# The mixers' output product: sixteen column products replaced by four column pairs in the seven-product scheme

## The chip, the cores and the metric

One core of one Trainium2 chip runs the kernel. The metric is the device time of one execution in microseconds (us); less is better. A core has five engines that run side by side, each through its own list of instructions in order: PE (TensorE, matrix products), DVE (VectorE), ACT (ScalarE), POOL (GpSimd) and SP (SyncE, which here only issues transfers). They wait for each other by semaphores.

## What is computed

One layer of a diffusion backbone over 1024 latent tokens and 256 context tokens, width 1024: a SwiGLU feed-forward half-step, then two mixers in parallel (a gated short convolution and grouped-query attention), merged by gates and sent through one output product, then a second feed-forward half-step. Cut to what matters here:

```python
x = x + 0.5 * ml[2] * swiglu(modulate(rms_norm(x, norm1_g), ml[0], ml[1]), ffn1_w_in, ffn1_w_out)
# mixers
merged = g_conv * (y_conv @ w_branch_conv) + g_attn * (o_attn @ w_branch_attn)     # 1024 x 1024
x = x + ml[5] * (merged @ w_out)                                                   # w_out 1024 x 1024
x = x + 0.5 * ml[8] * swiglu(modulate(rms_norm(x, norm3_g), ml[6], ml[7]), ffn2_w_in, ffn2_w_out)
return rms_norm(x, final_g)
```

The change concerns `merged @ w_out` and what stands just before and behind it.

## The kernel before

**Precision.** A float32 operand is split into two parts of a shorter format: the high part is a cast on ACT, the low part (the operand minus its high part) a subtraction on DVE. The function `split` issues both. A product of two operands is three matmuls: high by high, high by low, low by high (`mm3`, `terms`). Every matmul named below takes a 128x128 stationary operand and a 128x512 moving one.

**Layout.** Activations lie with their 1024 features in eight blocks of 128 partitions (index d, j or k) and their tokens in two halves of 512 columns, C0 and C1.

**The seven-product scheme.** The class `Winograd` multiplies a pair of 128-wide output columns of a weight (`pairs`) with both feature halves and both token halves in seven products instead of eight. Each product is 4 blocks x 3 matmuls = 12. The left operands (weights) are made in the generator `lefts`: it loads a raw tile of 512 KB per column (tag `raw`, three buffers), forms sums s1, s2, s3 and a second s2 on POOL, and splits each operand into a tile with the tag `wl` (four buffers). `prefetch` and `left` take from it. The right operands are eight lists `r[i]` of four tiles. Products 1 and 2 need only C0 (`norm0` makes `r[1]`, `r[2]` from the normalised C0: multiply by the broadcast of the norm on DVE into `h`, shift and scale on ACT, split). Products 6, 7, 4, 5, 3 need C1 too (`norm1`). `start` runs products 1 and 2 of the first nine pairs ahead (`AH3`), while `norm1` is made. The feed-forward inputs and the mixers' input use this class; the second feed-forward's instance is named `fast`.

**The stage in question**, after the attention heads, in the program's order:

1. `merge(j, ch)` for j = 0..7 and both halves: 24 matmuls of `w_ba` (the attention branch's weight) with the attention output (`o_parts`, tiles `oh` and `ol`), then on DVE `ga = ga * ps`, `ga = ga + z`, and a split into `m_hi`, `m_lo` (tiles `mh`, `ml`). The weight of one j is loaded and split once and kept for both halves. Two merges of C0 run between the last attention steps.
2. The output product: for C0 then C1, for each d, the weight column `w_out[:, d]` is loaded and split (`load_cols`: one 512 KB load, one ACT cast and one DVE subtraction of 128x1024), 8 x 3 = 24 matmuls follow, and one DVE operation adds the gated result to the residual `x` (tile `x2`, loaded from `xd`). So it has 2 x 8 x 24 = 384 matmuls.
3. `first = fast.norm0()` is stepped after the outputs d = 0, 1 and 2 of C1, so the norm of C0 and the right operands `r[1]`, `r[2]` of the second feed-forward are made while PE still has the outputs of C1 to do. `fast.square(d)` collects the squares of C1.

**Order.** A scheduler with its own model of times sets each engine's order when the program is built; the orders shown below are what it made. Buffers (38 tiles of 4 KB per partition in `apool`, 11 small ones in `tpool`) are handed on when their last reader is done.

Of the kernel before, what the change touches and what calls it, by code (L numbers as in the profile page):

```python
# [9 lines left out]
F32 = mybir.dt.float32  # L10
F32R = mybir.dt.float32r
# [38 lines left out]
def tile_dit_layer(  # L50
# [415 lines left out]
    class Winograd:  # L466
# [103 lines left out]

        def lefts(self, pairs, side_from):

            def cols(src):
                t = wpool.tile([P, SLOT], F32, tag="raw", name=uniq("raw"), bufs=3)
                load(t[:].rearrange("p (k n) -> p k n", n=P), src.rearrange("(k p) n -> p k n", p=P))
                return t[:, :512], t[:, 512:]
# [9 lines left out]
            def parts(src):  # L586
                tag = "wh" if self.side_from and self.n_left in WH else "wl"
                self.n_left += 1
                t = wpool.tile([P, 2, 512], F32R, tag=tag, name=uniq(tag), bufs=W_BUFS)
                split(src, t[:, 0], t[:, 1], self.lo_eng)  # L590
                return t
# [159 lines left out]
        def third(self, u, v):  # L751
# [5 lines left out]
            return u, v  # L757

# [727 lines left out]
    o_parts = [None] * NQ  # L1486

    def split_output(hd, *chunks):
        if o_parts[hd] is None:
            o_parts[hd] = atile("oh", dt=F32R), atile("ol", dt=F32R)  # L1490
        a, b = chunks[0][1], chunks[-1][1] + 512
        split(q_f[hd][:, a:b], *(t[:, a:b] for t in o_parts[hd]))
# [88 lines left out]
    m_hi, m_lo = {}, {}  # L1581
    wa = {}

    def merge(j, ch):

        if j not in m_hi:
            m_hi[j], m_lo[j] = atile("mh", dt=F32R), atile("ml", dt=F32R)
        if j not in wa:
            wa[j] = load_cols(w_ba[0], j * P)
        w, o = wa[j], ch[1]  # L1590
# [5 lines left out]
            (w[0][:, k], w[1][:, k], *(t[:, o : o + 512] for t in o_parts[k])) for k in range(KD)  # L1596
# [6 lines left out]
        dve.tensor_add(out=ga, in0=ga, in1=z)  # L1603
        split(ga, m_hi[j][:, o : o + 512], m_lo[j][:, o : o + 512])
# [265 lines left out]
```

## Time and profile before

| | |
|---|---|
| median of 3 runs | 2720.67 us (2720.63 to 2721.49) |
| the profiled execution | 2717.89 us, its span 2716.1 us |
| mean granted PE clock | 0.991 of full |
| PE busy | 2647.6 us (97%) |
| DVE / ACT / POOL busy | 2006.6 / 1167.2 / 532.1 us |

The profile is one execution. Its span runs from the first to the last instruction; the execution lasts 1.8 us longer than that, and the median run 2.8 us longer than the execution. Matmuls overlap each other, so a matmul's own duration is longer than the step from one start to the next; the step is what counts.

### The profile page before, as it was taken

Reading aid. Unit: us, or ns where it says so; the run is one execution under the profiler, and the core shown is the slowest. Engines: PE = TensorE matmul, PEld = TensorE weight load, DVE = VectorE, ACT = ScalarE, POOL = GpSimd, SP = SyncE. Lnnn points to the kernel's source line nnn. Section 1 sums busy time; section 2 is a strip of 40 time slices with the busy share of each in tenths; the row PEclk is TensorE's granted clock in tenths of the full one; section 3 lists DMA queues with packets and bytes.
Section 4 is the critical chain, followed back from the end, with each engine's and each line's share of the span. In section 5 each row is a group of like instructions: output and inputs, shape, how many; then the busy total and the mean of one; then the engine's idle time right before and its main releaser. Section 6 shows DMA issues by size and latency. Waiting matters only on the chain.

```text
span 2716.1 us, 37388 instructions
## 1 busy us (share of the span) xinstructions
PE 2647.6 (97%) x13593; PEld 2236.8 (82%) x13593; DVE 2006.6 (74%) x3356; ACT 1167.2 (43%) x2317; POOL 532.1 (20%) x409
## 2 busy tenths in 40 slices
PE   7999899999999999999999999999999999999998
PEld 4788798888778877888999888877888888888888
DVE  5889666988787899888478576685548876667885
ACT  5633443333443542333245665674226333334443
POOL 1244001221010043333033111100000442330100
PEclk9999999999999999999999999999999999999998
DMA  7665553445984345433312321001533552227831
GB/s 264 212 195 170 166 168 100 147 129 179 324 206 105 113 151 186 135 118 120 109 32 87 97 82 43 28 32 47 175 105 124 179 163 93 86 89 283 183 86 63
DMA packets 369922, 364.85 MB, mean 134 GB/s; under 512 B 27831, under 2 KB 261449, under 8 KB 369737
## 3 DMA queue, kind: packets, MB, share of 16 engines
q1 hardware_dynamic: 360712, 345.17, 38.5%
q0 software_dynamic: 9024, 17.30, 4.0%
q8 instruction: 106, 1.74, 0.3%
q14 instruction: 80, 0.65, 0.1%
HBM read 296.30 MB, written 66.06 MB: 133 GB/s over the span
## 4 chain that ended last, share of the span: by engine, by line
PE 55%; DVE 3%; ACT 1%; issue 0%; DMA 0%; DVEq 0%; ACTq 0%
PE ps L88 45%; PE pt L88 5%; PE po L88 4%; DVE xb L88 0%; DVE ol L88 0%; ACT pts L88 0%; DVE pts L88 0%; DVE wl L88 0%; DVE x L88 0%; DVE r L88 0%; ACT pl L88 0%; DMA y<-yd 0%; ACT q L88 0%; ACT oh L88 0%; DVE t L88 0%
## 5 line engine op out<-in xcount | busy, mean ns | idle before, releaser
L88 PE MATMUL ps<-r,wl 128*128 128x512 f32 x5232 | 1208.9, 391 | 14.9 <-ACT wl L88 7.9
L88 PEld LDWEIGHTS ps<-r,wl 128*128 128x128 f32 x5232 | 979.8, 188 | 223.1 <-ACT wl L88 10.0
L88 ACT CAST wl<-raw 128x512 fp32r<-128x512 f32 x286 | 176.9, 620 | 291.2 <-PE ps L88 191.6
L88 POOL TENSOR_TENSOR s<-raw 128x512 f32<-128x512 f32 x64 | 95.5, 1492 | 1011.0 <-DMA raw<-in_ffn_w_in_dram 641.7
L88 ACT CAST wl<-s 128x512 fp32r<-128x512 f32 x256 | 158.0, 620 | 315.1 <-PE ps L88 233.4
L88 DVE TENSOR_TENSOR wl<-raw,wl 128x512 fp32r<-128x512 f32 x284 | 198.6, 700 | 80.8 <-ACT wl L88 77.0
L88 DVE TENSOR_TENSOR wl<-s,wl 128x512 fp32r<-128x512 f32 x256 | 230.3, 900 | 12.6 <-ACT wl L88 11.6
L88 POOL TENSOR_TENSOR s<-raw,s 128x512 f32<-128x512 f32 x64 | 107.3, 1677 | 355.2 <-DVE wl L88 347.3
L88 DVE SCALAR_TENSOR_TENSOR macc<-rawm,silu_c,macc 128x512 f32<-128x512 f32 x168 | 141.0, 855 | 8.5 <-DMA rawm<-in_w_mod_dram 7.4
L88 PE MATMUL ps<-wh,r 128*128 128x256 f32 x768 | 141.6, 285 | 0.0
L88 DVE TENSOR_TENSOR pts<-pt,pts 128x512 fp32r<-128x512 f32 x160 | 108.8, 687 | 39.3 <-ACT pts L88 38.3
L88 DVE TENSOR_REDUCE m<-ps 128x1 f32<-128x512 f32 (+1 forms) x192 | 110.9, 596 | 31.1 <-PE ps L88 30.3
L88 DVE TENSOR_TENSOR u<-u,ps 128x512 f32<-128x512 f32 x168 | 114.1, 679 | 23.2 <-PE ps L88 22.9
L88 ACT CAST pts<-pt 128x512 fp32r<-128x512 f32 x160 | 93.2, 593 | 88.6 <-PE pt L88 86.7
L88 PE MATMUL ps<-rh,wl 128*128 128x512 f32 x360 | 123.7, 395 | 3.9 <-ACT rh L88 3.9
L88 ACT CAST rh<-hid 128x512 fp32r<-128x512 f32 x132 | 81.0, 620 | 103.4 <-PE ps L88 86.3
L88 PEld LDWEIGHTS ps<-wh,r 128*128 128x128 f32 x768 | 120.6, 192 | 0.0
L88 ACT CAST wh<-raw 128x512 fp32r<-128x512 f32 (+1 forms) x88 | 69.4, 796 | 100.5 <-PE ps L88 73.0
L88 PE MATMUL po<-pts,vh 128*128 128x512 f32 x256 | 110.6, 438 | 1.5 <-ACT pts L88 1.5
L88 PE MATMUL ps<-wl,r 128*128 128x256 f32 x384 | 108.8, 283 | 0.0
L88 DVE TENSOR_TENSOR rl<-hid,rh 128x512 fp32r<-128x512 f32 x132 | 89.9, 686 | 23.8 <-ACT rh L88 11.4
L88 PE MATMUL ps<-kl,qs 128*128 128x512 f32 x384 | 105.3, 397 | 0.0
(295 smaller groups left out, 5082.0 us busy)
## 6 DMA issues: line engine op xcount, KB each, us to landing
raw<-in_ffn_w_in_dram SPq DMA_DIRECT2D x125, 512.0 KB
raw<-in_ffn_w_out_dram SPq DMA_DIRECT2D x72, 512.0 KB
rawm<-in_w_mod_dram SPq DMA_DIRECT2D x128, 256.0 KB
raw<-in_w_in_dram SPq DMA_DIRECT2D x61, 512.0 KB
hid<-hd SPq DMA_DIRECT2D x40, 512.0 KB
ws<-in_ffn_w_out_dram POOLq DMA_DIRECT2D x30, 512.0 KB, 6.6
ucd<-uc SPq DMA_DIRECT2D x22, 512.0 KB
hd<-c SPq DMA_DIRECT2D x38, 256.0 KB
```

What stands on the lines that cost most here:

```text
L88: inst = getattr(self.engine, name)(*args, **kw)
```

## The change

- A class `OutColumns(Winograd)` computes `merged @ w_out` as four pairs of output columns in the seven-product scheme: 4 x 7 x 12 = 336 matmuls.
- The right operands are made inside `merge`. A merge of C0 writes a tile `h0` and splits it into `r[1]` or `r[2]`. Merges run all of C0 first, then C1 in the order 0, 4, 1, 5, 2, 6, 3, 7. After each second one of C1 DVE forms four differences (t1 to t4) and five splits follow (`r[6]`, `r[7]`, `r[4]`, `r[5]`, `r[3]`). Each merge loads and splits its own `w_ba` column, so 16 loads instead of 8.
- The left operands come from a `lefts` of its own: the four `wa` columns first (products 1 and 2 of all pairs), then per pair `wa` and `wb` again with four POOL sums. s1 and the second s2 of the pairs 1 and 2 go to the tag `wh`, to be used later.
- The products stand in the order: 1 and 2 of pairs 0 to 3 (`firsts`), then 6, 7, 4, 5, 3 of pair 0 (`seconds`, `thirds`), 6, 7, 4 of pairs 1, 2 and 3, then 5 and 3 of pairs 1, 2 and 3. Numbered in that order they are called p0 to p27 below.
- The results are added to `x2` per d and half as they come (`add2`), each with its square. The last result of C0 (d = 7) comes from p21. `fast.norm0()` is stepped behind `thirds(1)`, `thirds(2)` and `thirds(3)`.
- Attention outputs are split per half (`o_parts[hd, ch]`) instead of both halves at once for heads 0 to 6.

```diff
+        def part(self, src, tag="wl"):
+            t = wpool.tile([P, 2, 512], F32R, tag=tag, name=uniq(tag), bufs=W_BUFS)
+            split(src, t[:, 0], t[:, 1], self.lo_eng)
+            return t
...
+    class OutColumns(Winograd):
...
+        def lefts(self, pairs, side_from):
+
+            part, late = self.part, []
+            for wa, _ in pairs:
+                yield from map(part, self.cols(wa))
+            for j, (wa, wb) in enumerate(pairs):
+                a, b = self.cols(wa), self.cols(wb)
+                s1, s2, s3 = ttile("s1"), ttile("s2"), ttile("s3")
+                pool.tensor_add(out=s1, in0=b[0], in1=b[1])
+                pool.tensor_sub(out=s2, in0=s1, in1=a[0])
+                pool.tensor_sub(out=s3, in0=a[0], in1=b[0])
+                yield part(s2)
+                yield part(s3)
+                yield part(b[1])
+                pool.tensor_sub(out=s2, in0=a[1], in1=s2)
+                if 0 < j < len(pairs) - 1:
+                    late += part(s1, "wh"), part(s2, "wh")
+                else:
+                    yield from late if j else ()
+                    yield part(s1)
+                    yield part(s2)
...
+        def given(self, k, i, ch):
+
+            if ch == C0:
+                self.keep(1 + i, k, self.h0[k][:, i])
+            elif i:
+                f, h, t34, t1, t2 = self.h0[k], self.h1[k], atile("t34", (P, 2, 512)), ttile("nt"), ttile("nt")
+                b12, b22, t3, t4 = h[:, 0], h[:, 1], t34[:, 0], t34[:, 1]
+                dve.tensor_sub(out=t1, in0=b12, in1=f[:, 0])
+                dve.tensor_sub(out=t2, in0=b22, in1=t1)
+                self.keep(6, k, t2)
+                dve.tensor_sub(out=t3, in0=b22, in1=b12)
+                dve.tensor_sub(out=t4, in0=t2, in1=f[:, 1])
+                for r, t in ((7, t3), (4, t4), (5, t1), (3, b22)):
+                    self.keep(r, k, t)
...
     def merge(j, ch):
...
-        if j not in wa:
-            wa[j] = load_cols(w_ba[0], j * P)
-        w, o = wa[j], ch[1]
+        w, o = load_cols(w_ba[0], j * P), ch[1]
...
-        dve.tensor_add(out=ga, in0=ga, in1=z)
-        split(ga, m_hi[j][:, o : o + 512], m_lo[j][:, o : o + 512])
+        dve.tensor_add(out=merged.place(j % 4, j // 4, ch), in0=ga, in1=z)
+        merged.given(j % 4, j // 4, ch)
...
-    for j in range(KD):
-        for ch in (C0, C1):
-            if (j, ch) not in ((0, C0), (1, C0)):
-                run(merge(j, ch))
...
+    for j in range(2, KD):
+        run(merge(j, C0))
+    for j in (0, 4, 1, 5, 2, 6, 3):
+        run(merge(j, C1))
+    merged.prefetch(2)
+    run(merge(7, C1))
...
-    for ch in (C0, C1):
-        o = ch[1]
-        for d in range(KD):
-            w = load_cols(w_out[0], d * P)
-            load(xs(d, ch), xd[d, :, o : o + 512])
-            ps = ps_s()
-            mm3(ps, [
-                (w[0][:, k], w[1][:, k], m_hi[k][:, o : o + 512], m_lo[k][:, o : o + 512]) for k in range(KD)
-            ])
-            dve.scalar_tensor_tensor(
-                out=xs(d, ch), in0=ps, scalar=modl[:, 40 + d : 41 + d], in1=xs(d, ch), op0=ALU.mult, op1=ALU.add
-            )
-            if ch == C1:
-                fast.square(d)
-                if d in (0, 1):
-                    run(first, 1)
-                if d == 2:
-                    run(first)
+    def add2(d, ch, t):
+        load(xs(d, ch), xd[d, :, ch[1] : ch[1] + 512])
+        dve.scalar_tensor_tensor(
+            out=xs(d, ch), in0=t, scalar=modl[:, 40 + d : 41 + d], in1=xs(d, ch), op0=ALU.mult, op1=ALU.add
+        )
+        fast.square(d, ch)
...
+    run(merged.firsts())
+    for j in range(4):
+        add2(2 * j, C0, merged.uc[j][1])
+        add2(2 * j + 1, C0, merged.seconds(j))
+        if j == 0:
+            thirds(0)
+    thirds(1)
+    run(first, 1)
+    thirds(2)
+    run(first, 1)
+    thirds(3)
+    run(first)
```

**How the order moves, PE at the end of the stage.** Names: `ps` is a product's bank, `r` a right operand, `wl` a left one, `pt<-ident,rs_y` the broadcast of the norm of C0, on which `norm0`'s block waits. Before, the broadcast and, behind a row of output products, the last matmuls of the output product with the first ones of the second feed-forward:

```order
L88 MATMUL pt_19113<-ident,rs_y_19064 128x128 x4
...
L88 MATMUL ps_19314<-mh_18616,wh_19308 128x512
L88 MATMUL ps_19314<-ml_18617,wh_19308 128x512
L88 MATMUL ps_19314<-mh_18616,wl_19309 128x512
L88 MATMUL ps_19361<-r_3425_19124,wl_19347 128x512 x3
L88 MATMUL ps_19361<-r_3426_19129,wl_19347 128x512 x3
L88 MATMUL ps_19361<-r_3427_19134,wl_19347 128x512 x3
```

Now (p27 is `ps_19480`):

```order
L88 MATMUL ps_19480<-r_3388_18727,wl_19394 128x512 x3
L88 MATMUL ps_19480<-r_3412_18832,wl_19394 128x512 x3
L88 MATMUL pt_19436<-ident,rs_y_19382 128x128 x4
L88 MATMUL ps_19542<-r_3527_19447,wl_19528 128x512 x3
L88 MATMUL ps_19542<-r_3528_19452,wl_19528 128x512 x3
L88 MATMUL ps_19542<-r_3529_19457,wl_19528 128x512 x3
L88 MATMUL ps_19542<-r_3530_19462,wl_19528 128x512
L88 MATMUL ps_19584<-r_3535_19505,wl_19531 128x512
L88 MATMUL ps_19602<-r_3527_19447,wl_19536 128x512 x3
```

The broadcast stood 75 matmuls ahead of the second feed-forward's first; now it stands directly ahead of it.

**DVE at the same place.** `h<-x,pt` is the norm's multiplication, `r<-h,r` the low part of a right operand, `wl<-raw,wl` that of a left one. Before:

```order
L88 TENSOR_TENSOR h_3421_19118<-x_3357_18699,pt_19113 128x512
L88 SCALAR_TENSOR_TENSOR x_3393_18967<-ps_19206,modl,x_3393_18967 128x512
L88 TENSOR_TENSOR wl_19347<-raw_19345,wl_19347 128x512
L88 TENSOR_TENSOR h_3422_19119<-x_3362_18733,pt_19113 128x512
L88 TENSOR_TENSOR r_3425_19124<-h_3421_19118,r_3425_19124 128x512
L88 TENSOR_TENSOR h_3423_19120<-x_3367_18767,pt_19113 128x512
L88 TENSOR_TENSOR r_3426_19129<-h_3422_19119,r_3426_19129 128x512
L88 TENSOR_TENSOR h_3424_19121<-x_3372_18801,pt_19113 128x512
...
L88 TENSOR_TENSOR r_3427_19134<-h_3423_19120,r_3427_19134 128x512
```

Now:

```order
L88 TENSOR_TENSOR uc_18959<-uc_18959,ps_19480 128x512
L88 TENSOR_TENSOR h_3523_19441<-x_3442_18994,pt_19436 128x512
L88 TENSOR_TENSOR wl_19539<-raw_19534,wl_19539 128x512
L88 SCALAR_TENSOR_TENSOR x_3509_19359<-uc_18959,modl,x_3509_19359 128x512
L88 TENSOR_TENSOR h_3524_19442<-x_3456_19062,pt_19436 128x512
L88 TENSOR_TENSOR r_3527_19447<-h_3523_19441,r_3527_19447 128x512
L88 TENSOR_TENSOR sq_acc_19106<-sq_acc_19106,sq_19496 128x512
L88 TENSOR_TENSOR h_3525_19443<-x_3466_19114,pt_19436 128x512
L88 TENSOR_TENSOR r_3528_19452<-h_3524_19442,r_3528_19452 128x512
L88 TENSOR_TENSOR h_3526_19444<-x_3482_19189,pt_19436 128x512
...
L88 TENSOR_TENSOR r_3529_19457<-h_3525_19443,r_3529_19457 128x512
```

The block has the same shape (from the first `h` to the third low part `r` are 14 instructions in both), but it now stands behind the addition of the last product p27.

**DVE in the middle of the stage**, where left operands are made. Before (`wl<-raw,wh` is the low part of a whole output column's weight, `x<-ps` the addition of a result):

```order
L88 SCALAR_TENSOR_TENSOR x_3357_18699<-ps_18701,modl,x_3357_18699 128x512
L88 TENSOR_TENSOR wl_18831<-raw_18829,wh_18830 128x1024
L88 SCALAR_TENSOR_TENSOR x_3362_18733<-ps_18735,modl,x_3362_18733 128x512
L88 TENSOR_TENSOR wl_18864<-raw_18862,wh_18863 128x1024
L88 SCALAR_TENSOR_TENSOR x_3367_18767<-ps_18769,modl,x_3367_18767 128x512
```

Now, for pairs 2 and 3 (`ps_19158` is p14, `ps_19238` p17, `wl_19138` the left operand of p16, `wl_19218` that of p19; `s` are POOL's sums):

```order
L88 TENSOR_TENSOR wh_19202<-s_3473_19132,wh_19202 128x512
L88 TENSOR_TENSOR uc_18877<-uc_18877,ps_19158 128x512
L88 TENSOR_TENSOR wl_19138<-s_3474_19133,wl_19138 128x512
...
L88 TENSOR_TENSOR uc_18914<-uc_18914,ps_19238 128x512
L88 TENSOR_TENSOR wl_19218<-s_3491_19213,wl_19218 128x512
L88 TENSOR_TENSOR wl_19235<-s_3492_19214,wl_19235 128x512
```

A left operand now stands behind POOL's sums and behind the results of products two before it; SP's list has the loads of `x2` (thirteen, 256 KB each) between the raw columns of pair 1 and the second raw column of pair 2.

More of the change, by code (lines that the diff above doesn't have):

```diff
@@ L1481, in tile_dit_layer @@
     conv_weights(3)
-    o_parts = [None] * NQ
+    o_parts = {}
     def split_output(hd, *chunks):
[L1489 to L1492, printed above, removed]
+        for ch in chunks:
+            t = o_parts[hd, ch] = atile("o", (P, 2, 512), F32R)
+            split(q_f[hd][:, ch[1] : ch[1] + 512], t[:, 0], t[:, 1])
     class Unit:
@@ L1579, in seconds @@
             yield
[L1581 to L1582 removed]
+    merged = OutColumns([tuple(w_out[0][:, d * P : (d + 1) * P] for d in (e, e + 1)) for e in range(0, KD, 2)])
     def merge(j, ch):
[L1586 to L1590 removed]
+        w, o = load_cols(w_ba[0], j * P), ch[1]
         ga, z = ttile("ga"), ttile("z")
@@ L1595, in merge @@
         terms = [
-            (w[0][:, k], w[1][:, k], *(t[:, o : o + 512] for t in o_parts[k])) for k in range(KD)
+            (w[0][:, k], w[1][:, k], o_parts[k, ch][:, 0], o_parts[k, ch][:, 1]) for k in range(KD)
         ]
```

39 lines of the change are left out of this document (32 added, 7 removed).

## The prediction

> **What bounds the kernel now.** I read the page first, then the engines' busy time by stage, then the order of time of PE, DVE and ACT around the output product.
>
> ```profile
> span 2716.1 us, 37388 instructions
> PE 2647.6 (97%) x13593; PEld 2236.8 (82%) x13593; DVE 2006.6 (74%) x3356; ACT 1167.2 (43%) x2317; POOL 532.1 (20%) x409
> PE 55%; DVE 3%; ACT 1%; issue 0%; DMA 0%; DVEq 0%; ACTq 0%
> ```
>
> PE is busy for 97% of the span and carries the chain of work that ended last. Whether that holds in the stage itself is told by a table of three stretches: the merges, the output product, and the products that the second feed-forward runs ahead.
>
> ```profile
> core 0: us, PE busy (x) PEld busy (x) DVE busy (x) ACT busy (x) POOL busy (x), PEclk, DMA share, GB/s
> 1900.00:1964.00 64.00, 64.00 (x284) 53.01 (x283) 33.89 (x46) 15.35 (x20) 0.00 (x0) 1.00 0.49 158
> 1964.00:2052.00 88.00, 88.00 (x395) 73.00 (x394) 47.85 (x70) 32.55 (x45) 0.00 (x0) 1.00 0.36 113
> 2052.00:2102.00 50.00, 50.00 (x232) 41.65 (x231) 41.82 (x72) 29.75 (x51) 4.62 (x3) 1.00 0.42 137
> ```
>
> PE has no gap in any of them, at full clock (1.00), while DVE, ACT and the transfers have room. So a matmul less is time less, as long as PE does not come to wait. What one matmul costs is the step between starts. These rows are PE's in order of time: the last of the merges, the output product's first, one 29 later, the output product's last, and the second feed-forward's first.
>
> ```profile
> 1964.02 0.39 PE L88 MATMUL ps<-oh,wl 128*128 128x512 f32 x1
> 1964.24 0.39 PE L88 MATMUL ps<-mh,wh 128*128 128x512 f32 x1
> 1970.82 0.39 PE L88 MATMUL ps<-mh,wl 128*128 128x512 f32 x1
> 2052.48 0.39 PE L88 MATMUL ps<-mh,wl 128*128 128x512 f32 x1
> 2052.70 1.07 PE L88 MATMUL ps<-r,wl 128*128 128x512 f32 x4
> ```
>
> (1970.82 - 1964.24) / 29 = 0.227 us. A matmul shows 0.39 us of its own because they overlap. And between the output product and the next stage there is no seam: 2052.48 to 2052.70 is one step.
>
> **The change, part by part.**
>
> *Matmuls.* 384 become 336, so 48 steps of 0.227 us go: **-10.9 us**, all of it on PE's path.
>
> *The norm of C0 loses its cover: the first large term.* Before, its block on DVE and ACT ran beside output products. Rows of PE, DVE and ACT in order of time:
>
> ```profile
> 2035.24 0.60 PE L88 MATMUL pt<-ident,rs_y 128*128 128x128 f32 x4
> 2035.87 0.69 DVE L88 TENSOR_TENSOR h<-x,pt 128x512 f32<-128x512 f32 x1 [3.12 <-PE pt L88]
> 2037.10 0.81 ACT L88 ACTIVATE h<-h,modl,gain_l 128x512 f32<-128x512 f32 x1
> 2037.94 0.62 ACT L88 CAST r<-h 128x512 fp32r<-128x512 f32 x1
> 2038.56 0.82 ACT L88 ACTIVATE h<-h,modl,gain_l 128x512 f32<-128x512 f32 x1
> 2038.60 0.69 DVE L88 TENSOR_TENSOR r<-h,r 128x512 fp32r<-128x512 f32 x1
> 2040.67 3.07 DVE L88 TENSOR_TENSOR h<-x,pt 128x512 f32<-128x512 f32 x5
> 2044.32 0.68 DVE L88 TENSOR_TENSOR r<-h,r 128x512 fp32r<-128x512 f32 x1
> 2049.94 0.69 DVE L88 TENSOR_TENSOR r<-h,r 128x512 fp32r<-128x512 f32 x1
> 1964.44 0.69 DVE L88 TENSOR_TENSOR ga<-ga,ps 128x512 f32<-128x512 f32 x1 [2.65 <-PE ps L88]
> ```
>
> The first `h` comes 0.63 us after the broadcast starts; the third low part (2044.32) is done 2045.00 - 2035.87 = 9.13 us after the first `h` starts; the eighth and last (2049.94) 14.76 us after. Between broadcast and the next stage there were 17.5 us, so PE never noticed. Now the order puts the broadcast behind the last output product p27 and directly ahead of the products that need the block. Let 0 be the start of p27's last matmul. DVE adds p27's result first: 0.42 us after that start (1964.02 to 1964.44), for a step of 0.60 (five `h` in 3.07). So the first `h` starts at 1.02 (the broadcast alone would allow 0.23 + 0.63 = 0.86). DVE's list from there to the third low part has 14 instructions in both kernels (a square's sum stands for one addition to `x`), so I take the measured 9.13: third low part at 10.15. PE's list after p27 is: 4 transposes, then 3 matmuls for each of the first two pieces, the third piece's high part, and then its low part. So PE can do 0.23 + 0.36 + 7 x 0.227 = 2.2 us of work and stands for 10.15 - 2.2 = **8.0 us** in pieces. Behind that come 26 matmuls and 8 tiny ones before the eighth low part is wanted, at 10.15 + 26 x 0.227 = 16.0 us at the earliest; it is there at 1.02 + 14.76 = 15.8. So there is one wait, not two. Lower bound: 14 DVE steps of 0.60 without any wait for ACT give the third low part at 9.5, so 7.3 us. Upper bound: a block slower by 1 us, which the spare 0.2 us at its end does not absorb, 9.
>
> *What the wait does to the clock.* The trace has such waits elsewhere; rows of PE in order of time and of the busy time by stretch:
>
> ```profile
> 304.20 2.08 PE L88 MATMUL ps<-hidc,wo 128*128 128x256 f32 x8 [8.98 <-ACT wo L88]
> 308.00:310.00 2.00, 2.00 (x12) 2.00 (x12) 0.43 (x1) 0.62 (x1) 0.00 (x0) 0.61 0.00 0
> 1076.98 15.75 PE L88 MATMUL ps<-r,wl 128*128 128x512 f32 x60 [4.35 <-ACT wl L88]
> 1077.00:1078.00 1.00, 0.97 (x3) 0.52 (x4) 1.00 (x3) 1.00 (x3) 0.22 (x1) 0.79 0.68 262
> 1079.00:1080.00 1.00, 1.00 (x3) 0.77 (x3) 1.00 (x3) 0.01 (x1) 0.07 (x1) 0.50 0.01 2
> 1080.00:1081.00 1.00, 1.00 (x4) 0.75 (x3) 1.00 (x4) 0.00 (x0) 0.00 (x0) 0.51 0.63 182
> 1083.00:1084.00 1.00, 1.00 (x6) 0.79 (x6) 1.00 (x2) 0.00 (x0) 0.00 (x0) 1.00 1.06 323
> 973.00:974.00 1.00, 0.85 (x2) 0.13 (x1) 1.00 (x3) 1.00 (x3) 0.00 (x0) 0.50 0.00 0
> ```
>
> After 4.35 us of idleness the granted clock was 0.79, 0.50, 0.50, 0.51 in the next four microseconds, then 1.00: 0.21 + 0.50 + 0.50 + 0.49 = 1.7 us lost. After 8.98 us it was 0.50 from before the restart at 304.2 until about 309.2: 5.0 us at half speed, 2.5 lost. At 973 two matmuls between two waits ran at 0.50, so single matmuls do not hold the clock up. I take **+1.9 us** (nearest to the 4.35 case, since seven matmuls are spread over the wait; 0 and 2.6 are the ends). [...]
>
> *Left operands and POOL.* Pairs 1 to 3 now want three products (36 steps, 8.2 us) per two raw loads and four POOL sums. The second feed-forward runs the same making of operands at 19 us a pair. Rows of POOL and DVE in order of time, and of the busy time in one stretch:
>
> ```profile
> 2111.97 1.81 POOL L88 TENSOR_TENSOR s<-raw 128x512 f32<-128x512 f32 x1 [4.11 <-DMA raw<-in_ffn_w_in_dram]
> 2123.36 1.70 POOL L88 TENSOR_TENSOR s<-raw 128x512 f32<-128x512 f32 x1 [3.87 <-DMA raw<-in_ffn_w_in_dram]
> 2135.45 1.83 POOL L88 TENSOR_TENSOR s<-raw 128x512 f32<-128x512 f32 x1 [4.79 <-DMA raw<-in_ffn_w_in_dram]
> 2107.23 1.18 DVE L88 TENSOR_TENSOR wl<-raw,wl 128x512 fp32r<-128x512 f32 x1
> 1965.78 1.22 DVE L88 TENSOR_TENSOR wl<-raw,wh 128x1024 fp32r<-128x1024 f32 x1
> 2100.00:2120.00 20.00, 19.77 (x87) 15.73 (x86) 20.00 (x30) 13.13 (x24) 9.08 (x5) 1.00 0.46 156
> ```
>
> The ring of three raw buffers turns in 11.4 to 12.1 us there (2111.97, 2123.36, 2135.45): from the end of the second s2 it takes 3.9 to 4.8 us until the next pair's s1 starts. Working along the lists from p0's start (a product is 2.72 us): pair 0's b column can load when p1's operand buffer is free, at about 7, so s1 at 11.5; its buffer ring gives pair 1's s1 at 22 and s2 at 25 where p13 starts at 35.4: 9 us in hand. Pair 2's b column waits for pair 1's second s2 (30.5), so s2 is done at 38 to 39.6; its low part stands on DVE behind p14's result (41.0) and is ready at 42.3; p16 starts at 43.5. The second s2 of pair 2 then ends at 44.0, pair 3's s1 starts at 47.9 to 48.8, s2 ends at 50.6 to 52.2, and its two parts take about 1.4 us more (DVE beside POOL takes 1.18 instead of 0.68): 52 to 54. p19's third matmul wants it at 52.2. So **+1.0 us**, between 0 and 3. The thirteen loads of `x2` on SP's list ahead of pair 2's b column (3.3 MB, issued from 17.5 on) are through by about 33 at the 323 GB/s of the row at 1083, ahead of the time at which it is wanted.
>
> *What I cost at nothing.* Eight more `w_ba` loads and splits, four differences and the extra five-for-two splits per two merges of C1: DVE gets 15 instructions, two of them of 128x1024 (1.2 us, row at 1965.78), about 10 us per two merges (10.9 us of PE), where it had 33.9 of 64 us; the cover is PE's merges, and if DVE fell behind by more than the 11 us until p8 wants `r[6]`, PE would wait. The loads bring 1 MB per merge (5.4 us), 190 GB/s, where the stretch above moved 158 at a transfer share of 0.49. The two-halves splits of `o_parts` have the same elements. In the output product DVE has about 80 instructions of 0.6 us, 49 of 76 us, beside PE.
>
> *Given back later.* The norm of C1 in the feed-forward's first products now has 4 us more in hand, since PE starts them later by the wait. Before, PE stood 0.2 us there (19.77 of 20 at 2100 to 2120, DVE at 20.00): **-0.2 us**.
>
> Sum: -10.9 + 8.0 + 1.9 + 1.0 - 0.2 = **-0.2 us**. Made against the profiled execution (2717.89), that is 2717.7; the median run is 2.8 us above that execution, so I predict 2720.67 - 0.2 = **2720.5 us**: no change. This kernel's measurement tells from no change what is over about 0.2% (5.4 us).
>
> **Rivals.**
>
> *A, faster: the wait is mostly filled.* If PE needed only casts, the third high part would release it. ACT's shift and cast of a piece take 1.5 us (2037.10 to 2038.56), so three pieces, with two squares between them, end at 7.0; the wait is 4.9 us, the clock loses perhaps 0 to 1, operands 0: -10.9 + 4.9 - 0.2 = -6.2, **2714.5**. For it: PE does have further matmuls that need only early pieces. Against: PE keeps its list, and there the third low part stands ahead of them; on DVE four more `h` stand ahead of that. If the block stayed wholly hidden the time would be 2710; nothing supports it, because p27's addition stands ahead of the block.
>
> *B, slower: the left operands starve PE.* If the loads of `x2` hold pair 2's b column back so that it lands at 42 instead of 34 to 35, s2 comes at 45 and its parts at 46.5: p16 waits 3 us, and the ring hands the delay on to pair 3, whose parts come at 58 against p19 at 54.9: together 6 us. Instead of +1.0 that is +6, and with DVE slowed beside POOL +7: sum +5 to +6, **2726.5**. It decides from a landing of about 41 on. For it: the ring's 11.4 us against 8.2; against: 9 us in hand at pair 1, and transfers at a third of the share.
>
> *C, no gain from the scheme at all, in another way:* DVE falls behind in the merges of C1 and PE waits for weights there. [...]
>
> **How the numbers follow.** My forecast, with C: 0.72; A: 0.12; B: 0.16. Bounds of the unknown terms: lowest -10.9 + 7.3 + 0 + 0 - 0.2 = -3.8 (2716.9), highest -10.9 + 9 + 2.6 + 3 - 0.2 = +3.5 (2724.2). The range has to reach into A and B until less than 2 in 10 is out: 2714.5 to 2727. Faster by over 0.2% is A: 0.12; within: 0.72; slower: B, 0.16.
>
> **What would show it.** PE's step stays 0.227. PE's idle time has a group behind the low part of `r` of about 8 us at one place, just behind the broadcast `pt<-ident,rs_y`, with the granted clock at 0.50 for 3 to 5 us after it. The stretch of 28 products lasts 76 to 78 us. The merges show no wait of PE. Wrong would be: PE waiting for `wl` for more than 3 us in the stage (B), or a wait behind the broadcast of under 5.5 us (A).

## The result, and the profile after

The changed kernel takes 2726.58 us in the median of 13 runs (2718.94 to 2732.36); beside them the kernel before took 2720.97 us (13 runs, 2715.55 to 2723.81). The ratio is 1.0024, its 95% interval 1.0015 to 1.0033: slower by about 6.5 us (4.1 to 9.0). The forecast was no change (2720.5 us); the time lies just inside the upper end of its range, 2727 us.

The page of the changed kernel's profiled execution (2727.03 us):

```profile
span 2725.2 us, 37458 instructions
PE 2648.5 (97%) x13553; PEld 2234.7 (82%) x13553; DVE 2058.7 (76%) x3438; ACT 1186.6 (44%) x2360; POOL 554.8 (20%) x425
PE 53%; DVE 3%; ACT 1%; issue 1%; DMA 1%; POOL 0%; SPq 0%; DVEq 0%; POOLq 0%; ACTq 0%
```

PE is as busy as before (2648.5 against 2647.6 us) with 40 matmuls fewer (48 products' matmuls less, 8 tiny ones more), and DVE has 52 us more. The busy time by stretch (merges; p0 to p27; the seam behind p27; the second feed-forward's products ahead):

```profile
1900.00:1967.00 67.00, 67.00 (x298) 55.46 (x296) 48.18 (x69) 22.68 (x32) 0.00 (x0) 1.00 0.50 154
1967.00:2050.00 83.00, 80.31 (x352) 65.36 (x351) 65.14 (x101) 29.28 (x51) 23.40 (x16) 0.98 0.40 127
2050.00:2066.00 16.00, 10.04 (x27) 6.49 (x26) 13.33 (x22) 11.98 (x19) 0.00 (x0) 0.68 0.11 33
2066.00:2116.00 50.00, 49.78 (x229) 41.15 (x229) 43.71 (x75) 31.94 (x54) 6.49 (x4) 1.00 0.43 137
```

The merges have no gap of PE. In the output product PE has gaps and DVE works 65.1 of 83 us (47.9 of 88 before); at the seam PE works 10 of 16 us at a mean clock of 0.68.

**The seam.** PE in order of time, then stretches with the granted clock in the third column from the right:

```profile
2050.40 0.60 PE L88 MATMUL pt<-ident,rs_y 128*128 128x128 f32 x4
2053.83 0.49 PE L88 MATMUL ps<-r,wl 128*128 128x512 f32 x1 [2.83 <-ACT r L88]
2054.80 0.73 PE L88 MATMUL ps<-r,wl 128*128 128x512 f32 x2 [0.47 <-DVE r L88]
2056.24 2.37 PE L88 MATMUL ps<-r,wl 128*128 128x512 f32 x4 [0.71 <-ACT r L88]
2060.56 6.57 PE L88 MATMUL ps<-r,wl 128*128 128x512 f32 x17 [1.94 <-DVE r L88]
2066.97 0.28 PE L88 MATMUL pt<-ones,sq_acc 128*128 128x1 f32 x2
2068.67 1.65 PE L88 MATMUL ps<-r,wl 128*128 128x512 f32 x6
2055.00:2056.00 1.00, 0.53 (x2) 0.09 (x1) 0.94 (x2) 0.97 (x2) 0.00 (x0) 0.77 0.94 279
2056.00:2066.00 10.00, 7.81 (x17) 5.39 (x18) 7.38 (x12) 7.75 (x13) 0.00 (x0) 0.51 0.00 0
2066.00:2067.00 1.00, 1.00 (x7) 0.80 (x6) 0.00 (x0) 0.00 (x0) 0.00 (x0) 1.00 0.00 0
```

From the broadcast to 2068.67 PE issues 4 transposes, 24 matmuls and 16 tiny ones, 0.43 + 5.45 + 1.75 = 7.6 us of work, and takes 18.3: 10.6 us lost. The third low part lets PE go at 2060.56, 10.2 us behind the broadcast. Steps that are at least 0.3 us too long come to 8.2 us of waiting; the rest is the clock, which stood at half for about ten microseconds.

**The middle.** PE at p16 and p19, then the clock behind p16:

```profile
2011.06 0.73 PE L88 MATMUL ps<-r,wl 128*128 128x512 f32 x2 [0.38 <-ACT wl L88]
2013.69 10.31 PE L88 MATMUL ps<-r,wl 128*128 128x512 f32 x36 [1.90 <-DVE wl L88]
2024.41 3.46 PE L88 MATMUL ps<-r,wl 128*128 128x512 f32 x14 [0.41 <-DVE wl L88]
2014.00:2015.00 1.00, 1.00 (x5) 0.77 (x4) 1.00 (x2) 0.00 (x0) 1.00 (x1) 0.79 0.00 0
2016.00:2017.00 1.00, 1.00 (x4) 0.71 (x4) 1.00 (x2) 0.03 (x1) 0.00 (x0) 0.50 0.28 80
2018.00:2019.00 1.00, 1.00 (x6) 0.83 (x5) 0.84 (x2) 1.00 (x2) 0.00 (x0) 1.00 1.12 337
```

From the last merge's last matmul to the broadcast behind p27 the stage takes 2050.40 - 1967.22 = 83.2 us; before, up to the second feed-forward's first matmul, it took 2052.70 - 1964.02 = 88.7. The 88.7 us hold the broadcast's four transposes (0.4 us) and the 83.2 do not, so 5.1 us are saved instead of 10.9. The 5.8 us lost are 3.2 of waiting at p16 and p19, about 1.7 of half clock behind p16, and 0.9 for eight more tiny matmuls (C0's squares now stand in two sums; 0.11 us each). Middle and seam: -5.1 + 10.6 = +5.5 us; from the last merge to the end the profile gives 758.0 against 752.1 us, +5.9.

Why p16's left operand is late, by DVE, SP, POOL and again DVE:

```profile
1991.70 0.81 DVE L88 SCALAR_TENSOR_TENSOR x<-uc,modl,x 128x512 f32<-128x512 f32 x1 [3.63 <-DMA x<-xd]
1989.93 10.01 SPq L88 DMA_DIRECT2D x<-xd  x11
2001.72 4.60 SPq L88 DMA_DIRECT2D raw<-in_w_out_dram  x2
1999.89 1.80 POOL L88 TENSOR_TENSOR s<-raw,s 128x512 f32<-128x512 f32 x1 [4.52 <-DVE wl L88]
2006.04 1.68 POOL L88 TENSOR_TENSOR s<-raw 128x512 f32<-128x512 f32 x1 [4.35 <-DMA raw<-in_w_out_dram]
2007.79 1.63 POOL L88 TENSOR_TENSOR s<-s,raw 128x512 f32<-128x512 f32 x1
2007.20 1.06 DVE L88 SCALAR_TENSOR_TENSOR x<-uc,modl,x 128x512 f32<-128x512 f32 x1
2009.48 2.35 DVE L88 TENSOR_TENSOR sq_acc<-sq_acc,sq 128x512 f32<-128x512 f32 x2 [0.62 <-ACT sq L88]
2011.76 0.68 DVE L88 TENSOR_TENSOR wh<-s,wh 128x512 fp32r<-128x512 f32 x1
2012.36 0.67 DVE L88 TENSOR_TENSOR uc<-uc,ps 128x512 f32<-128x512 f32 x1
2012.96 1.28 DVE L88 TENSOR_TENSOR wl<-s,wl 128x512 fp32r<-128x512 f32 x2
```

DVE stands 3.6 us for the first load of `x2`. POOL's second s2 of pair 1 waits 4.5 us for DVE's split of the first, which it overwrites. When it ends, at 2001.69, pair 2's second raw column goes out (2001.72); SP had issued the last load of `x2` by 1999.94. Pair 2's s2 is done at 2009.4, and its low part starts on DVE at 2012.96, behind two sums of squares, another split and a result.

### The profile page after: what moved, and what is told of

The parts are those of the page before. It is cut to its first block, busy times and chain, and to the rows that moved or that the text cites. A ratio compares the mean times of both kernels' runs of the same rounds, so it can differ in the third digit from the quotient of the medians.

```text
span 2725.2 us, 37458 instructions
## 1 busy us (share of the span) xinstructions
PE 2648.5 (97%) x13553; PEld 2234.7 (82%) x13553; DVE 2058.7 (76%) x3438; ACT 1186.6 (44%) x2360; POOL 554.8 (20%) x425
## 4 chain that ended last, share of the span: by engine, by line
PE 53%; DVE 3%; ACT 1%; issue 1%; DMA 1%; POOL 0%; SPq 0%; DVEq 0%; POOLq 0%; ACTq 0%
PE ps L88 44%; PE pt L88 5%; PE po L88 4%; DVE xb L88 0%; POOL s L88 0%; DVE x L88 0%; DMA x<-xd 0%; DVE wl L88 0%; DVE o L88 0%; DVE m L88 0%; DVE pts L88 0%; DMA y<-yd 0%; DMA raw<-in_w_out_dram 0%; SPq L88 0%; ACT pts L88 0%
## 5 line engine op out<-in xcount | busy, mean ns | idle before, releaser
L88 PE MATMUL ps<-r,wl 128*128 128x512 f32 x5520 | 1284.0, 392 | 23.0 <-ACT wl L88 8.6
L88 PEld LDWEIGHTS ps<-r,wl 128*128 128x128 f32 x5520 | 1038.2, 189 | 247.1 <-ACT wl L88 10.4
L88 ACT CAST wl<-raw 128x512 fp32r<-128x512 f32 x298 | 184.6, 621 | 297.1 <-PE ps L88 200.1
L88 ACT CAST wl<-s 128x512 fp32r<-128x512 f32 x268 | 166.0, 621 | 324.8 <-PE ps L88 233.6
L88 DVE TENSOR_TENSOR wl<-raw,wl 128x512 fp32r<-128x512 f32 x296 | 208.3, 704 | 78.1 <-ACT wl L88 74.5
L88 DVE TENSOR_TENSOR wl<-s,wl 128x512 fp32r<-128x512 f32 x268 | 242.0, 904 | 19.6 <-ACT wl L88 18.0
L88 POOL TENSOR_TENSOR s<-raw,s 128x512 f32<-128x512 f32 x68 | 114.2, 1680 | 362.4 <-DVE wl L88 362.4
L88 DVE TENSOR_TENSOR pts<-pt,pts 128x512 fp32r<-128x512 f32 x160 | 109.2, 687 | 36.6 <-ACT pts L88 35.5
L88 POOL TENSOR_TENSOR s<-raw,raw 128x512 f32<-128x512 f32 x68 | 105.6, 1553 | 11.6 <-DVE wl L88 10.2
```

The lines of the kernel that those rows point to most:

```text
L88: inst = getattr(self.engine, name)(*args, **kw)
```

## Experiments

Each run was timed in five rounds against the kernel before. The waits are sums of what PE's steps exceed 0.23 us by (0.11 us behind a transpose; only steps over by at least 0.3, so a first step at half clock, up to 0.6 us, counts in), worked out from the starts of its matmuls in each profile: in the middle (p0 to p27; in late_squares_all with the wait for the squares), for rs_y ahead of the broadcast, behind it, and ahead of the second feed-forward's product 6. The last column is the time from the last merge to the end of the profiled execution, single executions that scatter by a few us.

| run | ratio to before (95%) | middle | rs_y | behind broadcast | product 6 | to the end |
|---|---|---|---|---|---|---|
| before | 1 | 0 | 0 | 0 | 0 | 752.1 |
| the change | 1.0024 (1.0015 to 1.0033) | 3.2 | 0 | 8.2 | 0.4 | 758.0 |
| x2_first | 1.0034 (1.0023 to 1.0046) | 4.8 | 0 | 8.3 | 0.3 | 759.1 |
| bcast_p26 | 1.0023 (1.0014 to 1.0032) | 4.0 | 2.3 | 3.9 | 3.0 | 761.2 |
| bcast_p25 | 1.0037 (1.0024 to 1.0049) | 3.8 | 3.6 | 0.3 | 6.3 | 762.8 |
| bcast_p25_x2_first | 1.0047 (1.0035 to 1.0060) | 5.4 | 3.5 | 0.3 | 7.0 | 765.0 |
| x2_on_act | 1.0029 (1.0019 to 1.0039) | 5.1 | 0 | 8.3 | 0 | 757.8 |
| norm_early | 1.0009 (1.0000 to 1.0017) | 3.0 | 2.8 | 1.6 | 3.0 | 756.5 |
| norm_early_ahead11 | 0.9992 (0.9984 to 1.0001) | 4.8 | 2.8 | 1.3 | 0 | 753.9 |
| norm_early_ahead11_x2_on_act | 1.0006 (0.9996 to 1.0017) | 3.3 | 2.8 | 1.6 | 0 | 748.6 |
| own_tile | 1.0019 (1.0010 to 1.0028) | 4.9 | 0 | 8.2 | 0 | 759.8 |
| norm_early_ahead11_own_tile | 0.9998 (0.9989 to 1.0006) | 4.1 | 2.8 | 1.3 | 0 | 751.9 |
| before_ahead11 | 0.9993 (0.9984 to 1.0001) | 0 | 0 | 0 | 0 | 751.3 |
| x2_between | 1.0017 (1.0007 to 1.0026) | 4.8 | 1.1 | 7.1 | 0 | 757.6 |
| x2_between_own_tile | 1.0024 (1.0015 to 1.0032) | 4.1 | 0 | 8.2 | 0 | 759.0 |
| norm_early_ahead11_x2_between_own_tile | 1.0000 (0.9991 to 1.0009) | 4.2 | 2.8 | 1.3 | 0 | 755.0 |
| no_sums | 1.0009 (1.0000 to 1.0018) | 1.4 | 0 | 7.8 | 0 | 753.6 |
| no_sums_x2_between_own_tile | 1.0010 (1.0000 to 1.0020) | 2.6 | 0 | 8.0 | 0 | 755.8 |
| late_squares_all | 1.0039 (1.0026 to 1.0052) | 8.1 | 0 | 4.8 | 0 | 761.1 |

**First: middle or seam, each with its simplest edit.**

```diff
 # x2_first
+    for d, ch in [...]:                  # all sixteen
+        load(xs(d, ch), xd[d, :, ch[1] : ch[1] + 512])
     run(merged.firsts())
 # bcast_p26: the first matmul of p26 is pinned behind the broadcast
     thirds(2)
     run(first, 1)
+    pin_next.append(True)
     thirds(3)
 # bcast_p25: the same between the two products of thirds(2)
-    thirds(2)
-    run(first, 1)
+    thirds(2, between=norm_here)         # run(first, 1), then pin the next matmul
```

What was expected of x2_first:

> All sixteen loads of x2 are traced ahead of p0 instead of one by one with the additions; nothing else changes. In the changed kernel DVE stood 3.63 us at an addition to x2 for its load, and p16 and p19 then stood about 2.6 and 0.6 us for left operands that are behind those additions on DVE. Theory M (the x2 loads hold DVE, and through it the left operands): the waits of p16 and p19 go, with the half clock behind p16, so 3 to 4.4 us less than the changed kernel, which is 2722 to 2723.5. Rival (DVE's backlog comes from POOL's sums beside it, the loads are innocent): within 1 us of the changed kernel. The seam behind p27 stays in both.

What was expected of bcast_p26:

> The first matmul of p26 is pinned behind the broadcast of the norm of C0, so the broadcast stands two products earlier on TensorE's list. Theory S (the block of the norm on DVE and ACT, exposed behind p27, and the half clock after it cost 10 to 11 us): the broadcast can start when rs_y is ready (2047.1 in the changed kernel's profile instead of 2050.4), so the third low part comes 3.3 us earlier, and more if DVE's list gets rs_y out sooner: 3 to 7 us less than the changed kernel, the wait behind the broadcast shorter by as much and split in two. Rival (the seam is due to left operands of the second feed-forward or the additions of C1, the broadcast only stands beside it): no change, within 1 us.

What was expected of bcast_p25:

> As the run with the broadcast ahead of p26, but one product earlier: ahead of p25, so three products (8.2 us) stand between broadcast and feed-forward. Theory S: the block of about 10 us is covered but for some 2 us; a wait of TensorE for rs_y of 1 to 3 us comes in its place ahead of p25: 6 to 10 us less than the changed kernel, so 2716.5 to 2720.5, and no half clock at the seam. Rival (the wait for rs_y eats what the cover gives): 0 to 3 us less.

What was expected of bcast_p25_x2_first:

> Both edits together: x2 loads first and the broadcast ahead of p25. If the middle (M) and the seam (S) are two separate losses they add up: 9 to 14 us less than the changed kernel, 2712.5 to 2717.5, faster than the kernel before. If they are one chain (a late middle makes the seam late as well), less than the sum of the two single runs by over 2 us.

All four missed the time that their theory gave; for bcast_p26 the rival's time came out (no change), but not its reason, since the wait behind the broadcast halved. In x2_first DVE no longer waits for a load and p16 waits 0.2 us, but the sixteen loads now stand ahead of pair 0's raw columns, and PE waits 2.9 us at p8 and 1.9 at p19: the time moved, and the run says nothing clean about theory M. The pinned broadcasts did shorten the wait behind them (8.2 to 3.9 to 0.3 us), which shows where the seam comes from; but it came back at two places. PE in bcast_p25:

```profile
2043.33 1.09 PE L94 MATMUL pt<-ident,rs_y 128*128 128x128 f32 x4 [3.46 <-DVE rs_y L94]
2111.51 5.06 PE L94 MATMUL ps<-r,wl 128*128 128x512 f32 x11 [5.80 <-ACT wl L94]
```

The first is the wait for rs_y: the sums of squares are on PE's list late, and DVE's short chain behind them stands between additions. The second is just ahead of product 6, where the norm of C1 is wanted: the row names the cast of product 6's left operand, which stands on ACT's list right behind eight casts of that norm's right operands. Both have to be moved as well.

**Second: the norm of C0 fully early, and more work ahead of the norm of C1.**

```diff
 # norm_early
     thirds(1)
     run(first, 1)
-    thirds(2)
-    run(first, 1)
+    pin_next.append(True)                # the sums stand ahead of p24
+    thirds(2, between=norm_here)         # the broadcast ahead of p25
 # ..._ahead11 and before_ahead11
-RESIDENT, AH2, AH3 = 2, 9, 9
+RESIDENT, AH2, AH3 = 2, 9, 11
 # x2_on_act
-        load(xs(d, ch), xd[d, :, ch[1] : ch[1] + 512])
+        act.dma_start(out=xs(d, ch), in_=xd[d, :, ch[1] : ch[1] + 512])
```

What was expected of norm_early:

> The sums of the norm of C0 are pinned ahead of p24 and its broadcast between p24 and p25, so that rs_y is out when TensorE gets there and three products stand behind it. In bcast_p26 and bcast_p25 TensorE waited 2.3 and 3.5 us for rs_y, and 3.0 and 6.0 us ahead of the second feed-forward's product 6. Theory S (the seam alone): the 8.2 us of waits behind p27 go, none comes in their place: 7 to 10 us less than the changed kernel, 2717 to 2720. Theory G (given back later: DVE has no time left between p21 and product 6, so the norm of C1 is as late as before): the waits move to a place just ahead of product 6, 4 to 7 us there; 0 to 3 us less than the changed kernel.

What was expected of norm_early_ahead11:

> As norm_early, and products 1 and 2 of eleven pairs instead of nine run ahead of the second feed-forward's norm of C1 (10.9 us more work of TensorE that does not need that norm). Theory G: the wait ahead of product 6 is covered, and the whole gain of norm_early comes out: 6 to 10 us less than the changed kernel, 2717 to 2721. If norm_early has no wait there (S alone), no change against norm_early. Rival (DVE is short in the whole stretch, and the two pairs bring it more work): under 2 us less than norm_early.

What was expected of before_ahead11:

> The kernel before with eleven pairs ahead instead of nine, and nothing else. It waited 0.2 us ahead of product 6, so theory G expects nothing of the edit here: within 1.5 us of the kernel before. Rival (the edit helps whatever the output product, by taking sums from GpSimd out of the stretch in which DVE is full): 2 to 4 us less, and then the gain of norm_early_ahead11 over norm_early is not the change's.

What was expected of x2_on_act:

> The sixteen loads of x2 go out on ScalarE's queue instead of SyncE's, so the raw columns have SyncE's list to themselves; TensorE's list is that of the changed kernel. In x2_first the waits of p16 were gone, but the raw columns came 6.6 us late. Theory M (x2 loads between the raw columns hold both the ring and DVE): pairs follow each other every 10 to 11 us from 13.4 us after p0's start, p16 and p19 do not wait, 3 to 5 us less than the changed kernel: 2721.5 to 2723.5. Rival (DVE's backlog beside POOL): p16 still waits for over 1.5 us, 0 to 1 us less.

What was expected of norm_early_ahead11_x2_on_act:

> All three edits. If seam, middle and norm of C1 are separate losses: 10 to 14 us less than the changed kernel, 2713 to 2717, faster than the kernel before by 4 to 8 us. If one of them takes over another's wait, within 2 us of norm_early_ahead11.

PE in norm_early (two rows) and in norm_early_ahead11 (one):

```profile
2044.23 1.03 PE L94 MATMUL pt<-ident,rs_y 128*128 128x128 f32 x4 [2.67 <-DVE rs_y L94]
2110.22 5.97 PE L94 MATMUL ps<-r,wl 128*128 128x512 f32 x24 [2.87 <-ACT wl L94]
2084.77 50.48 PE L94 MATMUL ps<-r,wl 128*128 128x512 f32 x222
```

Theory G has the mechanism, though not its sizes. With the seam's wait down from 8.2 to 1.6 us the time falls by 4 us (1.0024 to 1.0009), where the seam alone would have given 7 to 10 and theory G 0 to 3: 2.8 us go to rs_y and 3.0, not 4 to 7, to product 6. Two more pairs ahead take the wait at product 6 away (one row of 222 matmuls without a gap) and another 4.6 us by the ratios (0.9992). The control before_ahead11 has no such wait that the edit could take and still comes out at 0.9993, 1.9 us less; its interval (0.9984 to 1.0001) excludes neither no effect nor its rival's 2 to 4 us, so part of the 4.6 us may not be the change's. The changed scheme, mended this far, is level with the kernel before, and no better.

x2_on_act shows an edit that moves a hold instead of removing it. ACT's queue, ACT and POOL there:

```profile
1994.04 7.65 ACTq L88 DMA_DIRECT2D x<-xd  x5
2001.81 0.62 ACT L88 CAST wl<-s 128x512 fp32r<-128x512 f32 x1 [7.37 <-DMA x<-xd]
2003.23 1.74 POOL L88 TENSOR_TENSOR s<-raw,s 128x512 f32<-128x512 f32 x1 [6.75 <-DVE wl L88]
```

Five issues took 7.65 us on ACT's own list, where four just ahead, from 1987.91 on, took 1.77; the cast behind the five started after 7.4 us of idle time on ACT, which its row puts down to a transfer of `x2`, and behind it came DVE's split and POOL's second s2, which waited 6.75 us for that split because it overwrites s2. Why norm_early_ahead11_x2_on_act is 0.14% above norm_early_ahead11 although the waits in its profile are fewer stays open (its profiled execution took 2719.05 us, its median 2725.46 us).

**Third: what holds p16.** The second s2 in place, the loads of x2, or DVE itself.

```diff
 # own_tile
+                s4 = ttile("s4")
+                pool.tensor_sub(out=s4, in0=a[1], in1=s2)
                 yield part(s2)
...
-                pool.tensor_sub(out=s2, in0=a[1], in1=s2)
 # x2_between: loads pinned in the order of the additions, one ahead
-        load(xs(d, ch), xd[d, :, ch[1] : ch[1] + 512])
+        more_x2()
 # no_sums: in square(), for the second feed-forward
-            else:
+            elif self.m != 6:
                 dve.tensor_add(out=accs[0], in0=accs[0], in1=sq)
 # late_squares_all: C0's first six squares and two of C1, pinned
-        fast.square(d, ch)
+        if squared:
+            fast.square(d, ch)
```

What was expected of own_tile:

> The second s2 gets a tile of its own and stands right behind the first on GpSimd, so it no longer waits until DVE has split the first (it was written in place). In the changed kernel that wait was 4.5 us for pair 1, and the raw buffer that the second s2 reads was free, and the second raw column of pair 2 issued, only at its end (1999.89 + 1.78, and 2001.72). x2_on_act put a longer wait there (6.8 us) and p16 waited 4.7 instead of 2.6 us. Theory R (ring held by DVE through the tile written in place): that raw column goes out 4 us earlier, pairs follow each other every 10 to 11 us, p16 and p19 do not wait: 2.5 to 5 us less than the changed kernel. Rival (DVE's list is late by itself): p16 still waits over 1.5 us, under 1 us less.

What was expected of norm_early_ahead11_own_tile:

> norm_early_ahead11 with the tile of its own. If the middle is a loss of its own: 2.5 to 5 us less than norm_early_ahead11 (ratio 0.9992), so a ratio of 0.9973 to 0.9983, 2714.5 to 2718, faster than the kernel before. If DVE or the norms take it over: within 1 us of norm_early_ahead11, with a longer wait for rs_y or ahead of product 6.

What was expected of x2_between:

> The loads of x2 are pinned in the order in which the additions want them, one addition ahead, so SyncE's list has six of them ahead of pair 2's second raw column instead of sixteen, two behind it and eight behind pair 3's. The in-place second s2 stays. Theory X (that column is held twice: by the x2 loads ahead of it on SyncE and by the in-place s2 that frees its buffer): taking one hold away leaves the other, p16 still waits 1.5 to 3 us, within 1.5 us of the changed kernel (ratio 1.0019 to 1.0029). Rival (the x2 loads alone hold it): p16 does not wait, 3 to 5 us less.

What was expected of x2_between_own_tile:

> Both holds taken away: x2 loads between the raw columns, and a tile of its own for the second s2. Theory X: pair 2's second raw column goes out at about 26 us after p0's start instead of 34, its first sum comes at 31 to 33 instead of 38.8 and 40.1, p16 and p19 do not wait and the clock is not halved behind p16: 3.5 to 5.5 us less than the changed kernel, a ratio of 1.0003 to 1.0012. Rival (DVE's list is late by itself, which no transfer mends): p16 still waits over 1.5 us, under 1 us less.

What was expected of norm_early_ahead11_x2_between_own_tile:

> All of it: the norm of C0 pinned early, eleven pairs ahead, x2 loads between the raw columns, the tile of its own. If middle, seam and norm of C1 are three separate losses: 3 to 5 us less than norm_early_ahead11 (ratio 0.9992), so 0.9973 to 0.9982, faster than the kernel before and than before_ahead11. If one takes over another's wait: 0.9988 to 0.9995, with the wait for rs_y or ahead of product 6 longer.

What was expected of no_sums:

> The changed kernel without the additions of the squares on DVE (twelve additions of 0.7 to 1.7 us for both halves of x2; the norms of the second feed-forward then use two squares of eight, and the output is another). Theory D (DVE has no free time in the middle, so splits of left operands stand behind its additions and sums whatever the transfers do): the waits at p16 and p19 shrink from 3.2 to under 1.5 us in all; the seam stays at 7 to 9 us of waits; 2 to 5 us less than the changed kernel, a ratio of 1.0005 to 1.0016. Rival (the raw columns still come too late): p16 waits over 2 us, under 1.5 us less.

What was expected of no_sums_x2_between_own_tile:

> No additions of squares, and both holds of pair 2's raw column away (x2 loads between the raw columns, a tile of its own). In x2_between_own_tile the sums of pair 2 were ready 5 us earlier than in the changed kernel, and p16 still waited 4.1 us. Theory D: with DVE relieved as well no wait is left at p16 and p19: the 28 products take 76 to 79 us but for the seam, 4 to 6 us less than the changed kernel, a ratio of 1.0000 to 1.0010. Rival (something else makes p16 late): it still waits over 2 us.

What was expected of late_squares_all:

> A whole kernel again: the squares of C0 and of pair 0's C1 are pinned behind the making of all left operands, so DVE and ScalarE have them after the middle; with the norm early, eleven pairs ahead, x2 loads between the raw columns and the tile of its own. Theory D: p16 and p19 do not wait, but the eight additions now stand in the chain of the norm of C0, so the wait for rs_y grows from 2.8 us by 0 to 4 us: 0 to 4 us less than norm_early_ahead11, a ratio of 0.9977 to 0.9992. Rival (DVE has no room there either): the wait for rs_y grows by more than the middle gives, a ratio over 0.9995.

In own_tile (SP and POOL below) the second s2 no longer waits, but pair 2's raw column then waits behind the eleven loads of x2, and POOL for it:

```profile
1985.46 10.10 SPq L88 DMA_DIRECT2D x<-xd  x11
2003.44 1.29 POOL L88 TENSOR_TENSOR s<-raw 128x512 f32<-128x512 f32 x1 [11.34 <-DMA raw<-in_w_out_dram]
```

So there were two holds, and taking one away left the other: in x2_between p16 still waits 2.1 us and p19 2.7. x2_between_own_tile takes both, and decides between transfers and DVE. POOL, ACT, PE and DVE, and the busy time from p0 to p27:

```profile
2000.16 1.62 POOL L88 TENSOR_TENSOR s<-s,raw 128x512 f32<-128x512 f32 x1
2008.51 0.63 ACT L88 ACTIVATE sq_acc<-x 128x512 f32<-128x512 f32 x1 [5.01 <-DVE x L88]
2010.60 1.14 ACT L88 CAST wl<-s 128x512 fp32r<-128x512 f32 x2
2011.26 0.73 PE L88 MATMUL ps<-r,wl 128*128 128x512 f32 x2 [2.19 <-ACT wl L88]
2002.25 1.78 DVE L88 SCALAR_TENSOR_TENSOR x<-uc,modl,x 128x512 f32<-128x512 f32 x1
2003.95 1.27 DVE L88 TENSOR_TENSOR uc<-uc,ps 128x512 f32<-128x512 f32 x2
2007.02 0.67 DVE L88 TENSOR_TENSOR uc<-uc,ps 128x512 f32<-128x512 f32 x1
1965.00:2049.00 84.00, 80.17 (x352) 65.54 (x351) 68.78 (x101) 28.83 (x51) 24.41 (x16) 0.98 0.40 125
```

The last matmul of its last merge starts at 1965.23, so s2 is done 36.6 us later, against 42.2 in the changed kernel: 5.6 us earlier, nearly as expected. Yet p16 waits 4.1 us. ACT casts s2 9 us after it is ready, because its list has squares first, which wait for DVE's addition to x; and DVE is behind: it has no gap there, with additions of 1.78 us, and p12's result, whose last matmul starts at 2000.13, is added only at 2007.02. Theory X has the two holds right and what they cost wrong; its rival holds: DVE's list is late though the column is early. Part of that the edit brings with it: POOL's sums, no longer held, run beside more of DVE's work, and the same 101 instructions take 68.8 us instead of 65.1.

That DVE is late "by itself" is not shown. It stands 3.0 us for the first load of `x2` in this run too, and 1.6 to 3.6 us in every run of the changed scheme but the two with all loads first. In those two p16 waits 0.2 and 0.8 us, but PE had already lost over 2.4 us at p8. No run has that one load early and nothing else changed.

no_sums leaves out twelve additions on DVE, so that its output is another, and touches no transfer. PE in it:

```profile
2004.61 14.27 PE L88 MATMUL ps<-r,wl 128*128 128x512 f32 x60
2019.52 0.73 PE L88 MATMUL ps<-r,wl 128*128 128x512 f32 x2 [0.64 <-ACT wl L88]
2020.65 3.47 PE L88 MATMUL ps<-r,wl 128*128 128x512 f32 x14 [0.40 <-DVE wl L88]
```

p16 runs through, p19 waits 1.4 us; the middle's waits fall from 3.2 to 1.4 us, no half clock follows (the granted clock is 1.00 over 1967 to 2051, 0.98 in the changed kernel), and the ratio falls from 1.0024 to 1.0009, by about 4 us, as theory D expected. With the transfers' holds away as well it is no better (1.0010), and p16 waits 2.6 us, which theory D had excluded: ACT's squares still stand ahead of the cast, and POOL's sums now fall on more of DVE's work (91 instructions take 62.6 us; in no_sums 92 took 58.3). late_squares_all moves the sums instead of leaving them out, and loses (ratio 1.0039): p16 and p19 wait only 0.3 and 0 us, but p15 and p18 wait 1.6 and 1.7, and there are 4.4 us of waiting for the squares and 4.5 behind the broadcast. So the place behind the left operands is no better for them: there they stand in the chain of the norm. And with the norm early and eleven pairs ahead neither the tile of its own (0.9998) nor both edits (1.0000) gain on 0.9992, without the longer wait elsewhere that their rival named.

For the middle, then, it is shown that less work on DVE takes most of the loss away. How its lateness divides between the wait for `x2`, POOL beside it and the number of instructions is open.

## Why the prediction was wrong

- *Matmuls, -10.9.* Right: PE's step stayed 0.227 us, and the merges had no wait, so rival C did not occur (DVE was busy for 48.2 of 67 us there).
- *The norm of C0, +8.0.* Right in place and size: 8.2 us of waits just behind the broadcast, the third low part 10.2 us after it (10.15 was worked out).
- *The clock, +1.9.* Low by about 0.5: the seam cost 10.6 us in all, where 9.9 were forecast. The half clock did not end after 3 to 5 us; it held from about 2055.5 to 2065.8.
- *Left operands and POOL, +1.0 (0 to 3).* **This step failed**: 4.9 us (3.2 of waiting, 1.7 of half clock). The failing sentences are that p16's low part "stands on DVE behind p14's result (41.0) and is ready at 42.3", and that DVE has "about 80 instructions of 0.6 us, 49 of 76 us". DVE had 101 in 65.1 of 83 us. Counted from p0's start as there (1967.0), pair 1's second s2 ended at 34.7 instead of 30.5, since it waits for DVE's split; pair 2's s2 was done at 42.4 instead of 38 to 39.6 and the low part at 46.6. I followed that operand through the ring of raw buffers and past one result, and did not work out what else stands ahead of it on DVE's and ACT's lists, nor that DVE's split of one sum must free POOL's next.
- The eight more tiny matmuls, 0.9 us, were not in the sum. And SP's list had sixteen loads of `x2` ahead of pair 2's second raw column, not thirteen.
- *Given back later, -0.2.* A wait of 0.4 us stayed ahead of product 6, and it was that small only because the seam gave the norm of C1 its time. bcast_p25 showed 6.3 us there once the seam was shorter.

The sum comes to -10.9 + 10.6 + 4.9 + 0.9 = +5.5 us, against +5.9 between the two profiles and +6.5 by the ratio (4.1 to 9.0). Rival B had the place (p16 and p19), the sign and nearly the size (+6 for the operands, 2726.5 us), with a chance of 0.16; its mechanism was only half of it, and that its time came out within 0.1 us is luck, since it has the operands too dear and neither the tiny matmuls nor the rest of the half clock. The column came late, but it last waited for POOL's sum, not for the loads of `x2`; pair 2's first sum started 39.0 us after p0's start, ahead of the 41 from which B decided; and x2_between_own_tile shows that p16 waits even where s2 is done 5.6 us earlier.

The groups of DVE's work in the changed kernel's output product show the other half of DVE's load:

```profile
L88 DVE TENSOR_TENSOR uc<-uc,ps 128x512 f32<-128x512 f32 x23 | 15.3, 680 | 2.8 <-PE ps L88 2.8
L88 DVE TENSOR_TENSOR wl<-s,wl 128x512 fp32r<-128x512 f32 x12 | 11.8, 990 | 6.1 <-ACT wl L88 6.0
L88 DVE TENSOR_TENSOR sq_acc<-sq_acc,sq 128x512 f32<-128x512 f32 x11 | 8.6, 784 | 2.0 <-ACT sq L88 1.7
```

Additions with one operand from PE's bank kept their 0.68 us; additions and splits with both operands in the on-chip memory took 0.78 to 0.99 in the mean, up to 1.79 where POOL worked beside them and at most 0.75 where it did not.

## What to carry to other kernels

A product scheme with fewer matmuls pays in additions: before counting PE's saving, write out the whole list of the engine that makes and joins the operands (here 101 instructions for 28 products of 2.72 us), at the duration that it has beside the other engines, and look where a late operand stands in it. When a block loses its cover, shortening that wait alone moves it to the next consumer: here to the broadcast's own input and to the next norm, and the rest of the gain came only with work put ahead of that. Where an edit that removes one suspected hold changes nothing, look in its trace for the second hold before dropping the suspect.

## What the runs showed of the hardware

- The half clock at the seam lasted about 10 us (0.77 in 2055 to 2056, 0.51 over 2056 to 2066, 1.00 behind), although PE worked 7.8 of those 10 us in pieces. Behind p16, where PE worked without a gap from 2013.69 on, it lasted about 3.4 us (0.79 in 2014 to 2015, 0.50 over 2015 to 2018, 1.00 behind). What sets its length no run here tests.
- Transfers issued from ACT held ACT in x2_on_act: five issues took 7.65 us, where four just ahead took 1.77, and the cast behind the five started after 7.4 us of idle time.
